# A hybrid attention encoder: order of weight roundings, a later place for weight loads, and small edits at both ends

## The chip, the cores and the metric

The kernel runs on one core of one Trainium2 chip. The metric is the device time of one execution in microseconds. Before the change, three runs took 1371.48, 1372.12 and 1373.95 us; their median, 1372.12 us, is the time before.

The engines are called as in the profile: PE multiplies matrices, ACT, DVE and POOL work on vectors, and SP only issues transfers (DMAs). Each works through its own queue in order.

## The reference, cut to what matters

Two layers work on 512 tokens of width 1024, and a final norm follows. Each layer adds three things to x:

```
for l in range(DEPTH):                                   # DEPTH = 2
    x = x + hybrid_mixer(rms_norm(x, norm_mix[l]), ...)  # 8 neighbourhood heads || 8 grouped-query heads
    x = x + memory_cross_attention(rms_norm(x, norm_mem_q[l]), rms_norm(mem, norm_mem_kv[l]), ...)
    x = x + conv_ffn(rms_norm(x, norm_ffn[l]), ...)      # SwiGLU, width-3 convolution, 2816 channels
return rms_norm(x, norm_final)
```

The neighbourhood attention (NA) has windows of 8 x 16 on an 8 x 64 grid of tokens, with a learned bias. The grouped-query attention (GQA) has 8 query heads on 2 key heads, with normed and rotated queries and keys. The memory attention has 4 heads over 256 memory tokens. All inputs are float32.

## The kernel before, in words

**Splitting.** A matmul takes operands in a rounded 32-bit format (`fp32r`). To keep float32's accuracy each operand is split into a rounded part `hi` and a rest `lo`, and each product is three matmuls (`mm3`): hi·hi, hi·lo, lo·hi. So each weight tile goes through three steps: a DMA of the raw tile on SP's queue (`emit_raw`), a rounding copy on ACT (`act.copy`, L290), and a subtraction, on POOL for nearly all tiles and on DVE for a few (`tensor_sub`, L291). There are two raw buffers and four pairs of `hi` and `lo`. A raw buffer comes free when the subtraction has read it, and the DMA for the next tile, which waits for that, holds up SP's queue.

**Plan and prefetch.** `plan` lists the weight tiles of the whole run in order of use. `get_w(key)` hands out the next one; before that it splits tiles until two (`AHEAD`) lie ready beyond it, and issues raw loads until two more (`N_RAW`) are on their way.

**Order.** PE's and SP's instructions stay in program order (`InOrder`, `Counted`). ACT's, DVE's and POOL's are ordered by a planner, which simulates a timeline and takes what is ready there, by priority: `behind(n)` gives a later rank (negative: an earlier one), and `tc.issue_after(ins)` forces an instruction behind another on its engine. The roundings have rank `behind(45)`, and `follow()` forces them behind the first of the reads of PSUM by ACT (`read(...)`) that were traced since the `get_w` before. The roundings of some tiles are forced behind the last closing row of x instead (`closed`), and those of `w_up` and `w_down` are not forced.

**Stages of a layer.** First some steps of projections (`attn_fill.step(N_FIRST[l])`: 7 in layer 0, 16 in layer 1; a step of a query or key projection is 6 matmuls of 512 columns, one of a value projection 12 of 256 columns). Then a weave of the NA units (8) and one of the GQA units (16), whose scores, softmax, transposes and value products are interleaved on PE with the remaining projections as filler. Then the rest of the filler, the memory attention with its own weave, and the feed-forward part in three groups of channels. `late(n, fn)` puts off a piece of program text until PE has been given n times 3.6 us of estimated work (`LATE = 3600`): so come the copies of each key half to the other half of the partitions (`double`, `r<-r`, two DMAs), the value blocks that straddle two tiles (`straddle`, `r<-r`, five DMAs), the swap for the rotation (`t<-t`, four DMAs) and others.

**Banks.** PSUM has four `mm` banks (projections, value products), two `sc` (scores) and two `tr` (transposes, statistics). `mem_stat`, in layer 0's NA weave, computes the memory's norm with two `tr` banks.

**The start.** `FIRST` gives the order in which chunks of x and pieces of the first three weights are loaded. ACT's queue issues the first norm's gains (`par`), then the first pieces of weights 0 and 1; SP's queue issues the rest. Six products of `ident` warm PE up.

**The end.** `down_last` works in two halves of 256 tokens. After the last row of a half its norm's `stat` sums the squares of the first seven chunks with PE, then those of the last one; then come a power on POOL, `spread` (products with `ident` that spread the result over the partitions), the scaling and the stores.

Of the kernel before, what the change touches and what calls it, by code (L numbers as in the profile page):

```python
# [13 lines left out]
ALU = mybir.AluOpType  # L14
# [4 lines left out]
P = 128  # L19
S = 512  # L20
D = 1024
# [7 lines left out]
MB = MEMN // P  # L29
# [3 lines left out]
EPS = 1e-6  # L33
# [16 lines left out]
MEM_FILL = [1, 1, 2, 2, 1, 3, 1, 3, 1, 3, 1]  # L50
N_ROWS = 3
LATE = 3600
W_BEHIND, N_RAW, N_W, AHEAD, AHEAD_HELD, N_WARM, N_LATE, N_FIRST = 45, 2, 4, 2, 5, 6, 4, (7, 16)


class InOrder:
# [113 lines left out]
def weave(n, steps, filler, quanta):  # L170


    last = max(st[0] for st in steps if st)
    for s in range(n + last):
        pieces = iter(quanta(s))
        for st in steps:
            if st is None:
                filler(next(pieces))
            elif 0 <= s - st[0] < n:
                st[1](s - st[0])  # L180
# [3 lines left out]
def encoder_kernel(ctx: ExitStack, tc: tile.TileContext, t: dict, out: bass.AP):  # L184
    nc = tc.nc
    PE, SP = Counted(tc, nc.tensor), InOrder(tc, nc.sync)
    late = Late(PE)
    ACT_IN_ORDER = InOrder(tc, nc.scalar)
    ACT, DVE, POOL = Free(nc.scalar), Free(nc.vector), Free(nc.gpsimd)
# [9 lines left out]
    @contextmanager  # L199
    def behind(n):  # L200


        at = tc.cur_priority
        tc.cur_priority = at + n
        yield
        tc.cur_priority = at
# [30 lines left out]
    ps_mm = lambda: ps("mm", 4)  # L237
    ps_s = lambda: ps("sc", 2)
    ps_t = lambda: ps("tr", 2)
# [6 lines left out]
    closed = []  # L246


    reads, marks = [], [0, 0]

    def read(e):
        reads.append(e.ins)
# [1 line left out]

    def follow():
        at = marks[-2]
        return tc.issue_after(reads[at]) if at < len(reads) else nullcontext()

    def raw_tile():
        key, loads, nk, ncol, eng = plan[len(raws)]  # L260
# [7 lines left out]
    def emit_raw():  # L268
        raw, loads = raw_tile()
        for dst, src in loads:  # L270
            SP.dma_start(dst(raw), src)
# [22 lines left out]
    def get_w(key, ahead=AHEAD):  # L294
        n = done[0]
        assert plan[n][0] == key, (plan[n][0], key)
        marks.append(len(reads))
        ahead = n + 1 + ahead
        while ahead < min(len(plan), n + 1 + AHEAD_HELD) and plan[ahead][4][1:] == "r":
            ahead += 1  # L300
        while len(ready) < min(len(plan), ahead):
            while len(raws) < min(len(plan), len(ready) + N_RAW):
                emit_raw()
            emit_split()
        while len(raws) < min(len(plan), len(ready) + N_RAW):
            emit_raw()
        done[0] += 1
        w = ready[n]
        ready[n] = None
        return w  # L310
# [73 lines left out]


    FIRST = [0, (0, 0, 2), 1, (1, 0, 2), 2, (0, 2, 4), 3, (1, 2, 4), (2, 0, 4), 4, (0, 4, 8), 5, (1, 4, 8), (2, 4, 8), 6, 7]
    nc.scalar.dma_start(par[:, 0, 0:8], t["par"][:, 0, 0:8])
    first_loads = []
    for n in FIRST:
        if isinstance(n, int):  # L390
            SP.dma_start(xT[n], t["xT"][n * P : (n + 1) * P, :])
            continue
        u, k0, k1 = n
        if u == len(first_loads):
            first_loads.append(raw_tile())
        raw, loads = first_loads[u]
        (nc.scalar if u < 2 and k0 == 0 else SP).dma_start(raw[:, k0:k1], loads[0][1][:, k0:k1])
    ACT_IN_ORDER.copy(small(1), ones)
    qkg = cpool.tile([P, DEPTH, 2], F32, name="qkg")
    gfin = cpool.tile([P, KC], F32, name="gfin")  # L400
# [37 lines left out]
    class Norm:  # L438
# [41 lines left out]
                eng.tensor_add(self.acc, self.acc, sq)  # L480
            return e

        def stat(self, factor=1.0):
            nb = self.n // P

            def sums(sq):
                pv = ps_t()
                for b in range(nb):
                    PE.matmul(pv[:, b : b + 1], sq[:, b * P : b * P + P], ones, start=True, stop=True)
                return pv[:, 0:nb]  # L490

            if self.last is None:
                self.rstd, self.var = rsqrt(sums(self.acc), nb, 1.0 / D, factor)
                return

            part, v, self.rstd = small(nb), small(nb), small(nb)
            DVE.tensor_scalar(part, sums(self.acc), 1.0 / D, EPS, op0=ALU.mult, op1=ALU.add)
            DVE.scalar_tensor_tensor(v, sums(self.last), 1.0 / D, part, op0=ALU.mult, op1=ALU.add)
            POOL.tensor_tensor(self.rstd, v, mhalf[:, :nb], op=ALU.pow)

        def spread(self, copy=ACT.copy):
# [65 lines left out]
    def mem_stat():  # L567

        acc = None
        for i in range(KC // 2):  # L570
            sq = tmp((2, MEMN))
            SP.dma_start(sq, t["memT"][i * 256 : (i + 1) * 256, :].rearrange("(k p) n -> p k n", p=P))
            yield
            ACT.activation(sq, sq, AF.Square)
            if acc is None:
                acc = sq
            else:
                POOL.tensor_add(acc, acc, sq)
        POOL.tensor_add(acc[:, 0], acc[:, 0], acc[:, 1])
        yield  # L580
        pv = ps_t()
        for b in range(MB):
            PE.matmul(pv[:, b : b + 1], acc[:, 0, b * P : (b + 1) * P], ones, start=True, stop=True)
        v = small(MB)
        DVE.tensor_scalar(v, pv[:, 0:MB], 1.0 / D, EPS, op0=ALU.mult, op1=ALU.add)
        POOL.tensor_tensor(mem_rstd, v, mhalf[:, :MB], op=ALU.pow)
        yield
        pr = ps_t()
        for b in range(MB):
            PE.matmul(pr[:, b * P : (b + 1) * P], mem_rstd[:, b : b + 1].to_broadcast([P, P]), ident,  # L590
                      start=True, stop=True)
        with behind(-30):
            ACT.copy(mem_rep, pr[:, :MEMN])
        yield

    warm = ps_t()
    for _ in range(N_WARM):
        PE.matmul(warm[:, 0:P], ident, ident, start=True, stop=True)  # L600
    nn = Norm(G_MIX, 0)
    DVE_IN_ORDER = InOrder(tc, nc.vector)
    for n in FIRST:
# [3 lines left out]
        u, k0, k1 = n  # L607
# [22 lines left out]
    for l in range(DEPTH):  # L630
# [465 lines left out]
        def na_quanta(s):  # L1096
# [4 lines left out]
            if s == 3:  # L1101
# [2 lines left out]
                gqa_eps()  # L1104
            return [NA_FILL] * 3

        weave(8, [(2, na_transpose), None, (1, na_normalise), (0, na_scores), None, (2, na_values), None], attn_fill.run, na_quanta)
        weave(4 * NB, [(2, gqa_transpose_p), (1, gqa_normalise), (0, gqa_scores), (3, lambda u: gqa_values(u, 0)),
                       (4, lambda u: gqa_values(u, 1)), None], attn_fill.pace, lambda s: [GQA_SLOT[s]])
        attn_fill.finish()  # L1110
        nn = nns[0]

# [184 lines left out]
        def down_last(g):  # L1297

            j0, nj = GROUPS[g]
            ops = [acts.pop(j) for j in range(j0, j0 + nj)]  # L1300
            ws = []

            def scale(half, m):
                xc = xT[m][:, 256 * half : 256 * half + 256]
                DVE.tensor_scalar(xc, xc, gfin[:, m : m + 1], 1.0, op0=ALU.mult, op1=ALU.mult)

            def finish(norm, last=False):
                norm.spread()
                y = [rtile((4, 256), F32) for _ in range(2)]
                for k in range(KC):  # L1310
                    yk, xk = y[k // 4][:, k % 4], xT[k][:, norm.cols]
                    if k in (2, 5):
                        POOL.tensor_mul(yk, xk, norm.rep)
                    else:
                        DVE.tensor_mul(yk, xk, norm.psum)
                for i, (k, n) in enumerate(((0, 2), (2, 2), (4, 2), (6, 1), (7, 1))):
                    (ACT_IN_ORDER if last and i % 2 else SP).dma_start(
                        out[k * P : (k + n) * P, norm.cols].rearrange("(k p) n -> p k n", p=P), y[k // 4][:, k % 4 : k % 4 + n])

            norms = []  # L1320
            for half in range(2):
                cs = slice(256 * half, 256 * half + 256)
                hops = [(hi[:, cs], lo[:, cs]) for hi, lo in ops]
                norms.append(Norm(cols=cs))
                rows = []
                for m in range(KC):
                    if half == 0:
                        ws.append(get_w(("down", g, m)))
                    rows.append(ps_mm()[:, :256])
                    late = half == 0 and m < N_LATE  # L1330
                    gemm_T(rows[m], ws[m], hops, range(nj - 1 if late else nj), 0, nj - 1)
                    for i in [m] if not late else range(N_LATE) if m == N_LATE - 1 else []:
                        if late:
                            gemm_T(rows[i], ws[i], hops, [nj - 1], 0, nj - 1)
                        DVE.tensor_add(xT[i][:, cs], xT[i][:, cs], rows[i])
                        norms[half].square(i)
                        scale(half, i)
                    if half == 1 and m == 1:
                        norms[0].stat()
                    elif half == 1 and m == 3:  # L1340
                        finish(norms[0])
            norms[1].stat()
            finish(norms[1], True)

        for g, (j0, nj) in enumerate(GROUPS):
# [96 lines left out]
```

## Time and profile before

| | us |
|---|---|
| median of three runs | 1372.12 |
| the profiled execution | 1373.07 |
| its span, first to last instruction | 1371.3 |
| PE busy | 1347.8 |
| DVE, POOL, ACT busy | 881.6, 688.4, 675.3 |

In this profile a row of the timeline has the start, the length, the engine and line of the program, the operation, what it writes and reads, its shape and count; brackets show how long the engine was idle before it and what ended that. A wait is listed as the one who waits, the one that released it, the total in us, the number of times and the longest. A busy time by stretch has the stretch, its length, then the busy time of PE, PEld (weight load), DVE, ACT and POOL with counts, the granted share of the PE clock, the share of the DMA engines and GB/s. A DMA issue has the size and the median time until it landed. Most float32 products have two records for each instruction.

### The profile page before, as it was taken

The numbers are of one execution on the slowest core, as the hardware profiler recorded it, in microseconds if no ns is written. First come the engines' busy times: TensorE is split into PE (matmuls) and PEld (weight loads), VectorE is DVE, ScalarE is ACT, GpSimd is POOL, SyncE is SP. The second block draws the span as 40 slices with busy tenths as digits, with TensorE's granted clock in tenths as the row PEclk, the third lists the DMA queues.
The fourth block names the chain that finished last, engine by engine and source line by source line (L and its number), as shares of the span: only waits on it lengthen the run. The fifth ranks groups of instructions, "written<-read, shape, count | busy, mean of one in ns | idle before, by whom it ended". The sixth has DMA issues, their size and how long they took to land.

```text
span 1371.3 us, 19217 instructions
## 1 busy us (share of the span) xinstructions
PE 1347.8 (98%) x7068; PEld 1154.7 (84%) x7068; DVE 881.6 (64%) x1542; ACT 675.3 (49%) x1258; POOL 688.4 (50%) x491
## 2 busy tenths in 40 slices
PE   9999999999999999999989999999999999999997
PEld 7888899878888888888878888998788888888897
DVE  6677775665885288177436677746758834862874
ACT  6776676555542244243447667756554422432441
POOL 2467756627444444443734576657264444444451
PEclk9999999999999999999999999999999999999998
DMA  6763213313333332432355441132143333323321
GB/s 214 208 187 102 59 47 93 108 46 104 97 92 98 102 93 81 118 93 81 100 148 174 137 116 54 59 97 93 32 123 92 99 101 93 100 85 108 96 89 62
DMA packets 219358, 139.88 MB, mean 102 GB/s; under 512 B 6144, under 2 KB 212224, under 8 KB 219264
## 3 DMA queue, kind: packets, MB, share of 16 engines
q1 hardware_dynamic: 218160, 137.99, 34.1%
q8 instruction: 56, 0.92, 0.3%
q10 hardware_dynamic: 1104, 0.66, 0.2%
q14 instruction: 38, 0.31, 0.1%
HBM read 126.05 MB, written 2.10 MB: 93 GB/s over the span
## 4 chain that ended last, share of the span: by engine, by line
PE 89%; ACT 4%; DVE 3%; DMA 2%; issue 1%; SPq 0%; ACTq 0%; POOL 0%; DVEq 0%
PE mm L77 79%; PE sc L77 6%; PE tr L64 3%; PE tr L77 1%; ACT t L790 1%; DMA r<-r 1%; ACT hi L290 1%; DMA t<-in_memT 1%; DMA xT<-in_xT 0%; DVE sc L784 0%; DVE t L480 0%; DMA raw<-in_w_in 0%; ACT t L1145 0%; DVE r L727 0%; ACT r L725 0%
## 5 line engine op out<-in xcount | busy, mean ns | idle before, releaser
L291 POOL TENSOR_TENSOR lo<-raw,hi 128x1024 fp32r<-128x1024 f32 (+2 forms) x268 | 500.3, 1877 | 486.5 <-ACT hi L290 471.9
L77 PE MATMUL mm<-xg,hi 128*128 128x512 f32 x1920 | 595.2, 391 | 0.0
L77 PEld LDWEIGHTS mm<-xg,hi 128*128 128x128 f32 x1920 | 355.7, 188 | 70.1
L77 PE MATMUL mm<-xg,lo 128*128 128x512 f32 x960 | 373.8, 389 | 0.0
L290 ACT CAST hi<-raw 128x512 fp32r<-128x512 f32 (+2 forms) x276 | 224.2, 836 | 297.8 <-PE mm L77 251.7
L77 PE MATMUL mm<-r,hi 128*128 128x512 f32 (+1 forms) x1096 | 316.3, 373 | 0.0
L77 PEld LDWEIGHTS mm<-r,hi 128*128 128x128 f32 x1096 | 198.3, 189 | 34.5 <-DVE r L507 0.4
L1266 DVE SCALAR_TENSOR_TENSOR t<-t,par,t 128x7 f32<-128x7 f32 (+1 forms) x352 | 202.0, 641 | 34.0 <-ACT t L1259 34.0
L77 PEld LDWEIGHTS mm<-xg,lo 128*128 128x128 f32 x960 | 180.2, 188 | 38.2
L77 PE MATMUL mm<-r,lo 128*128 128x512 f32 (+1 forms) x548 | 203.6, 372 | 0.0
L77 PEld LDWEIGHTS mm<-r,lo 128*128 128x128 f32 x548 | 103.3, 188 | 18.0
L1251 DVE TENSOR_TENSOR t<-mm,rep 128x512 f32<-128x512 f32 x88 | 60.1, 687 | 78.7 <-PE mm L77 62.4
L513 POOL TENSOR_SCALAR t<-t,s 128x512 f32<-128x512 f32 (+1 forms) x112 | 66.7, 611 | 81.6 <-DVE s L796 41.7
L1272 DVE TENSOR_TENSOR r<-t,r 128x512 fp32r<-128x512 f32 x44 | 90.4, 2054 | 7.3 <-ACT r L1271 4.1
L1268 ACT ACTIVATE t<-t 128x512 f32<-128x512 f32 x44 | 27.8, 633 | 134.5 <-DVE t L1266 134.4
L1295 DVE TENSOR_TENSOR xT<-xT,mm 128x512 f32<-128x512 f32 x32 | 21.9, 686 | 106.8 <-PE mm L77 106.8
L77 PE MATMUL sc<-r,r 128*128 128x256 f32 (+1 forms) x352 | 71.6, 336 | 4.9 <-DMA r<-r 4.4
L1259 ACT ACTIVATE t<-t,par 128x512 f32<-128x512 f32 x88 | 66.8, 806 | 3.3 <-DVE t L1251 3.3
L64 PE MATMUL tr<-ident,t 128*128 128x128 f32 x456 | 61.5, 273 | 5.7 <-DVE t L513 3.9
L64 PEld LDWEIGHTS tr<-ident,t 128*128 128x128 f32 x456 | 52.5, 140 | 14.5 <-issue 6.0
L77 PE MATMUL mm<-r,r 128*128 128x256 f32 (+1 forms) x428 | 62.2, 297 | 1.3 <-DMA r<-r 1.3
L77 PEld LDWEIGHTS sc<-r,r 128*128 128x128 f32 x352 | 52.6, 193 | 9.8 <-DMA r<-r 4.4
(154 smaller groups left out, 1624.2 us busy)
## 6 DMA issues: line engine op xcount, KB each, us to landing
raw<-in_w_up SPq DMA_DIRECT2D x88, 512.0 KB, 3.7
raw<-in_w_in SPq DMA_DIRECT2D x33, 512.0 KB, 4.1
raw<-in_w_down SPq DMA_DIRECT2D x32, 448.0 KB, 3.7
raw<-in_w_mem_kv SPq DMA_DIRECT2D x16, 512.0 KB, 3.9
raw<-in_w_down SPq DMA_DIRECT2D x16, 512.0 KB, 3.9
r<-in_bias SPq DMA_DIRECT2D x16, 384.0 KB, 5.5
r<-r SPq DMA_DIRECT2D x22, 256.0 KB, 5.6
raw<-in_w_out SPq DMA_DIRECT2D x8, 512.0 KB, 4.2
```

The lines of the kernel that those rows point to most:

```text
L64: return lambda *a, **k: self.tc.keep_in_program_order(op(*a, **k))
L77: return self.tc.keep_in_program_order(self.engine.matmul(out, lhsT, rhs, **k))
L290: act.copy(hi[:, k], raw[:, k])
L291: (POOL if eng[0] == "P" else DVE).tensor_sub(lo[:, k], raw[:, k], f(hi)[:, k])
L513: eng.tensor_scalar(e, e, sums[:, col : col + 1], 1.0, op0=ALU.mult, op1=ALU.mult)
L790: ACT.activation(es[j][:, i, :], sc[j][:, i, :], AF.Exp, bias=nmx[:, col], scale=-1.0, accum_out=sums[:, col])
L1251: DVE.tensor_mul(u, us[side], ffn.rep)
L1259: ACT.activation(cc, u, AF.Identity, bias=par[:, l, CB + ch : CB + ch + 1], scale=w[1])
L1266: DVE.scalar_tensor_tensor(cc[:, dst], u[:, src], wi, cc[:, dst], op0=ALU.mult, op1=ALU.add)
L1268: ACT.activation(cs[0], cs[0], AF.Silu)
L1272: DVE.tensor_sub(acts[j][1], cs[0], f(acts[j][0]))
L1295: DVE.tensor_add(xT[m], xT[m], pm)
```

## The change

- `follow()` forces the roundings only while `woven[0]` is true, that is during the two weaves of the attentions; before, it did so everywhere outside the feed-forward part.
- During the weaves `get_w` no longer issues its last raw loads at once, but with `late(1, load)`; what a split needs is still loaded before it.
- `mem_stat` takes `mm` banks instead of `tr` banks, and its first DVE operation gets an earlier rank.
- The first piece of weight 0 is issued on ACT's queue before `par`; the first piece of weight 1 moves to SP's queue, behind the second chunk of x.
- 7 warm-up products instead of 6; in layer 0, 8 steps of projection before the NA weave instead of 7.
- In the last norm three products of `ident` follow the sums of the first seven chunks and three more the sums of the last.

```
-W_BEHIND, N_RAW, N_W, AHEAD, AHEAD_HELD, N_WARM, N_LATE, N_FIRST = 45, 2, 4, 2, 5, 6, 4, (7, 16)
+W_BEHIND, N_RAW, N_W, AHEAD, AHEAD_HELD, N_WARM, N_LATE, N_FIRST = 45, 2, 4, 2, 5, 7, 4, (8, 16)
...
-    reads, marks = [], [0, 0]
+    reads, marks, woven = [], [0, 0], [False]
...
     def follow():
         at = marks[-2]
-        return tc.issue_after(reads[at]) if at < len(reads) else nullcontext()
+        return tc.issue_after(reads[at]) if woven[0] and at < len(reads) else nullcontext()
...
-        while len(ready) < min(len(plan), ahead):
+        def load():
             while len(raws) < min(len(plan), len(ready) + N_RAW):
                 emit_raw()
+
+        while len(ready) < min(len(plan), ahead):
+            load()
             emit_split()
-        while len(raws) < min(len(plan), len(ready) + N_RAW):
-            emit_raw()
+
+        if woven[0]:
+            late(1, load)
+        else:
+            load()
...
-    nc.scalar.dma_start(par[:, 0, 0:8], t["par"][:, 0, 0:8])
...
-        (nc.scalar if u < 2 and k0 == 0 else SP).dma_start(raw[:, k0:k1], loads[0][1][:, k0:k1])
+        (nc.scalar if n == FIRST[1] else SP).dma_start(raw[:, k0:k1], loads[0][1][:, k0:k1])
+        if n == FIRST[1]:
+            nc.scalar.dma_start(par[:, 0, 0:8], t["par"][:, 0, 0:8])
...
-        def stat(self, factor=1.0):
+        def stat(self, factor=1.0, warm=lambda: None):
...
             DVE.tensor_scalar(part, sums(self.acc), 1.0 / D, EPS, op0=ALU.mult, op1=ALU.add)
+            warm()
             DVE.scalar_tensor_tensor(v, sums(self.last), 1.0 / D, part, op0=ALU.mult, op1=ALU.add)
+            warm()
...
-        pv = ps_t()
+        pv = ps_mm()
...
-        DVE.tensor_scalar(v, pv[:, 0:MB], 1.0 / D, EPS, op0=ALU.mult, op1=ALU.add)
+        with behind(-30):
+            DVE.tensor_scalar(v, pv[:, 0:MB], 1.0 / D, EPS, op0=ALU.mult, op1=ALU.add)
...
-        pr = ps_t()
+        pr = ps_mm()
...
+    def warm_up(n):
+
+        warm = ps_t()
+        for _ in range(n):
+            PE.matmul(warm[:, 0:P], ident, ident, start=True, stop=True)
+
+    warm_up(N_WARM)
...
+        woven[0] = True
         weave(8, ...)
         weave(4 * NB, ...)
+        woven[0] = False
...
-            norms[1].stat()
+            norms[1].stat(warm=lambda: warm_up(3))
```

More of the change, by code (lines that the diff above doesn't have):

```diff
@@ L594, in mem_stat @@
         yield
-    warm = ps_t()
-    for _ in range(N_WARM):
-        PE.matmul(warm[:, 0:P], ident, ident, start=True, stop=True)
+    def warm_up(n):
[3 more added lines that the diff above has]
+    warm_up(N_WARM)
     nn = Norm(G_MIX, 0)
```

## The prediction

> **What bounds the kernel now.** I read the page first, then PE's waits, then each longer wait in the timeline, then the granted clock beside it.
>
> ```profile
> PE 1347.8 (98%) x7068; PEld 1154.7 (84%) x7068; DVE 881.6 (64%) x1542; ACT 675.3 (49%) x1258; POOL 688.4 (50%) x491
> PE sc L77 <- DMA r<-r: 4.4, 2, 4.2
> PE tr L64 <- DVE t L513: 3.9, 4, 1.6
> PE mm L77 <- DMA r<-r: 1.3, 1, 1.3
> ```
>
> TensorE is busy for 98% of the span, so no other engine's load matters as such, and the change adds nothing to PE's work but seven small warm-up products. What it can win or lose lies in the other 2%: the list of PE's waits (microseconds in total, times, longest) names the pieces of it, and the work of the others counts only where it ends one of them. The largest is one wait of 4.2 us for an `r<-r` transfer, at the start of layer 1's attentions:
>
> ```profile
> 710.33 0.80 PE L77 MATMUL sc<-r,r 128*128 128x256 f32 x2 [4.24 <-DMA r<-r]
> 711.35 1.62 PE L77 MATMUL sc<-r,r 128*128 128x256 f32 x6 [0.21 <-DMA r<-r]
> 710.33:715.40 5.07, 4.85 (x21) 4.59 (x22) 1.68 (x8) 3.12 (x9) 2.47 (x2) 0.52 0.51 150
> 715.40:720.00 4.60, 4.60 (x41) 4.60 (x40) 0.66 (x2) 1.64 (x5) 1.39 (x3) 1.00 0.97 255
> ```
>
> The first two rows are of the timeline (start, length, engine and line; in brackets PE's idle time before and what ended it), the others are busy times by stretch, where the third number from the end is the granted clock. The wait costs more than itself: afterwards the clock is 0.52 for 5.07 us. In that stretch 21 matmuls ran; at the 4.60/41 = 0.112 us of the next stretch they would take 2.36, so 5.07 - 0.21 - 2.36 = 2.5 us go to the slow clock. The whole event is worth 4.24 + 0.21 + 2.5 = 6.95 us, 0.5% of the run.
>
> **Term A, the roundings before layer 1's attentions: -6.4 us.** Why was that transfer late?
>
> ```profile
> 696.07 1.18 ACT L707 CAST r<-sc 64x512 fp32r<-64x512 f32 x2
> 699.83 1.18 ACT L725 CAST r<-mm 64x512 fp32r<-64x512 f32 x2 [2.59 <-DVE mm L693]
> 701.03 1.14 ACT L290 CAST hi<-raw 128x512 fp32r<-128x512 f32 x2
> 701.73 2.55 POOL L291 TENSOR_TENSOR lo<-raw,hi 128x512 fp32r<-128x512 f32 x2 [11.86 <-ACT hi L290]
> 697.66 1.41 DVE L711 TENSOR_TENSOR r<-sc,r 64x512 fp32r<-64x512 f32 x2
> 688.92 9.10 SPq L64 DMA_DIRECT2D raw<-in_w_in  x2
> 697.65 7.02 SPq L64 DMA_DIRECT2D raw<-in_w_in  x2
> 705.07 1.17 SPq L64 DMA_DIRECT2D r<-r  x2
> raw<-in_w_in SPq DMA_DIRECT2D x33, 512.0 KB, 4.1
> ```
>
> The key halves to be doubled were written by DVE at 699.07 (697.66 + 1.41). Their transfers stand on SP's queue behind a raw weight load that waits for its buffer, that is for POOL's subtraction, which ends at 704.28; the subtraction waits for the rounding at 701.03, and POOL had idled 11.86 us. The rounding was tied behind the read at 699.83. These are steps 1 to 16 of layer 1, before the two weaves, where the tie now goes. The weight's load was issued at 688.92 and a load of this kind lands after 4.1 us (the last row, from the list of DMA issues), so at 693.0. Free of the tie, the rounding either starts then (POOL done at 693.0 + about 0.6 for the first half + 2.55 = 696.2, the doubling issued when its source is ready, 699.1) or after the reads of 696.07, at 697.3 (POOL done at 700.5, doubling at 701.3, as 705.07 follows 704.28 by 0.8). The doubling lands about 5.2 us after issue (705.07 to 710.33, less a little): 704.3 or 706.5. PE asks at 706.1 (710.33 - 4.24). So nothing remains, or some 0.4 us, and about as much again for the second half (the two doublings share the 1.17 us of issue), without a slow clock: gain 6.95 or 6.0, taken 6.4; bounds 0 (the order stays) and 6.95. Next late would be the second key's doubling, which is needed only by the next head pair, after PE has gone through another stretch of fill. One untied rounding in layer 0's first steps comes back in term G. Outside the weaves the tie also goes in the memory attention, term D. In the up and down projections it was never used.
>
> **Term B, raw loads a step later in the weaves: -1.3 us.** Per weight one load of 0.37 us issue moves by 3.6 us of PE work, behind the key doublings, value straddles, query swaps, bias and memory loads that are queued in that time. One wait shows the price of the old order:
>
> ```profile
> 768.30 2.54 POOL L291 TENSOR_TENSOR lo<-raw,hi 128x512 fp32r<-128x512 f32 x2
> 770.86 0.37 SPq L64 DMA_DIRECT2D raw<-in_w_in  x1
> 771.33 3.26 SPq L64 DMA_DIRECT2D r<-r  x5
> 777.05 1.22 PE L77 MATMUL mm<-r,r 128*128 128x256 f32 x6 [1.29 <-DMA r<-r]
> ```
>
> Five straddles stand behind a load that waited for POOL until 770.84. Two of the five read the first half of the values, ready long before, so they can leave early and the other three follow some 1.3 us sooner, with no 512 KB load ahead of them. Bounds 0 and -1.3, the whole wait; taken -1.3, since SP had nothing else to do between. The cover of the later loads is the slack of the weights, weighed below as a rival.
>
> **Term C, the memory statistic in `mm` banks: -0.9 us.**
>
> ```profile
> 85.44 0.63 PE L64 MATMUL tr<-ident,t 128*128 128x128 f32 x4 [1.09 <-DVE s L585]
> 96.90 0.33 PE L64 MATMUL tr<-ident,t 128*128 128x128 f32 x1 [0.28 <-ACT mem_rep L593]
> 83.43 0.48 DVE L510 SCALAR_TENSOR_TENSOR r<-mm,s,r 128x256 fp32r<-128x256 f32 x1 [1.07 <-ACT r L509]
> 85.77 0.87 DVE L838 TENSOR_TENSOR t<-mm,t 64x256 f32<-64x256 f32 x2
> ```
>
> The two waits, 1.37 us, are for `tr` banks held by the statistic; they go. But when the statistic's products come, just ahead of the transposes and so near 83.4, the four `mm` banks are all held: two by the value products (read by DVE until 86.6), one by a projection in progress, one until 83.91. So the statistic would wait 0.5 us itself, with transposes and projection queued behind it on PE. Bounds -1.4 and +0.5.
>
> **Term D, roundings in the memory attention: -1.2 us.**
>
> ```profile
> 288.75 0.33 DVE L513 TENSOR_SCALAR s<-s,s 128x1 f32<-128x1 f32 x2
> 288.83 0.59 ACT L506 CAST r<-tr 128x512 fp32r<-128x512 f32 x1 [1.68 <-PE tr L64]
> 289.31 1.05 ACT L290 CAST hi<-raw 128x1024 fp32r<-128x1024 f32 x1
> 290.27 0.56 ACT L1145 ACTIVATE t<-sc,s,s 128x256 f32<-128x256 f32 x1
> 293.16 0.63 PE L64 MATMUL tr<-ident,t 128*128 128x128 f32 x4 [1.60 <-DVE t L513]
> ```
>
> The exponent was ready at 289.08 and ran at 290.27, after a tied rounding of 1.05 us; the transposes then waited 1.60, and as much again once more (the four waits for L513 sum to 3.9, the longest 1.6), which I read as the same place in layer 1. ACT had 1.68 us idle before 288.83, room for that rounding. If it moves there, 1.2 us return in each layer; if it lands before another exponent, up to 1.05 is lost. Half of 2.4 is taken; bounds -3.2 and +1.1.
>
> **Term E, the warm end: -0.5 us.**
>
> ```profile
> 1350.42 0.60 PE L77 MATMUL tr<-ident,s 128*128 128x128 f32 x4
> 1362.12 0.61 PE L77 MATMUL tr<-ones,t 128*128 128x1 f32 x4 [0.68 <-ACT t L469]
> 1363.76 1.22 PE L77 MATMUL tr<-ident,s 128*128 128x128 f32 x4 [1.03 <-POOL s L499]
> 1363.70:1365.00 1.30, 1.22 (x4) 0.93 (x4) 0.00 (x0) 0.00 (x0) 0.00 (x1) 0.52 0.00 0
> ```
>
> The same four records took 0.60 at 1350.42 and 1.22 at the end, at clock 0.52. Three products of two records are some 0.7 to 0.9 us (0.60/4 x 6), put into gaps of 0.68 and 1.03. The first set may overrun by 0.2, and DVE, POOL, ACT and the stores all follow it. Bounds -0.6 and +0.2. The Trainium skill ("TensorE: Matmul & The Clock Gate", section "HAM oscillation — how this bites in real kernels") says that the clock survives idle gaps under about 3.4 us; by that rule these gaps need no warming and the term would be 0, the time 1362.7. The row disagrees: the clock was halved after gaps of 0.68 and 1.03. After the 4.24 us gap of term A rule and row agree.
>
> **Terms F and G, the beginning: -0.1 and +0.5 us.**
>
> ```profile
> 17.16 6.48 DVE L480 TENSOR_TENSOR t<-t,t 128x512 f32<-128x512 f32 x6
> 37.70 0.95 PE L77 MATMUL sc<-r,r 128*128 128x256 f32 x6 [0.48 <-DVE r L713]
> 39.03 0.38 PE L77 MATMUL mm<-hi,xg 128*128 128x256 f32 x1 [0.39 <-DVE r L727]
> ```
>
> F: the first weight piece leaves ACT's queue one issue sooner, the norm's gains behind it one later, and the second weight piece moves to SP's queue, behind two chunks of x. Whatever PE saves is taken back by the sum of squares, which DVE ends at 23.64 and PE already awaits: -0.1, bounds -0.3 and +0.3. The seventh warm-up product lies in PE's idle time. G: one more half block of values (twelve products of some 0.12 us, 1.4 us) before the weave covers the 0.48 wait, but the block that now waits 0.39 us for a bank, freed just before 39.03, then comes before the scores, which begin some 0.4 us ahead of that 0.48 wait, near 36.8; it waits up to 2.2 us, 1.3 more than the two waits now. A rounding of 1.14 us, untied, may leave ACT's reads of the same stretch and shorten that. Bounds -0.9 and +1.5; taken +0.5.
>
> Sum: -6.4 - 1.3 - 0.9 - 1.2 - 0.5 - 0.1 + 0.5 = -9.9 us. The profiled execution took 1373.07 us, 0.95 above the median 1372.12 of the runs shown, so the median is forecast at 1362.2.
>
> **Rivals.** First, the order stays: the untied rounding is still put behind the read of the second query (699.83), because ACT's order is a planner's. Then A is 0 and the time 1368.6. For it: the planner gives these roundings a late rank. Against: ACT idles 2.59 us before 699.83.
>
> Second, on the other side, weights come too late. SP's loads slip by 3.6 us and by what is now ahead of them:
>
> ```profile
> 57.56 0.37 SPq L64 DMA_DIRECT2D raw<-in_w_in  x1
> 66.92 2.55 POOL L291 TENSOR_TENSOR lo<-raw,hi 128x512 fp32r<-128x512 f32 x2
> 75.55 0.40 PE L77 MATMUL mm<-hi,xg 128*128 128x256 f32 x2
> ```
>
> This load is of the second half of a value weight, first used near 75.6; its low part is done at 69.47, a slack of 6.1 us. With ten projections in each layer, a slip of 7.5 us would cost 1.4 us at each of 20: +28, time 1390. It decides from a slip of 6.1 + (9.9 + 2.7)/20 = 6.7 us. Against: landed by 61.7 (57.56 + 4.1), this weight lies there for 5 us before its subtraction, so most of a slip is absorbed ahead of the slack; and no wait of PE for POOL's low parts stands in the list of before.
>
> **Numbers.** Forecast 0.69 (1357.5 to 1366); order stays 0.13 (faster, 1368.6); small losses of C, D and G eat most, without A, 0.06 (within 0.2%, 2.7 us, about what a measurement can tell); late weights 0.12 (slower). Faster 0.82. All good ends together are -14.7, 1357.4; the range 1357.5 to 1369.5 holds the first two cases and leaves out the last two.
>
> **What would show it.** A: no `sc` wait for `r<-r` near 705 and clock 1.00 there; B: none at 775; C: no wait for L585, perhaps one for a `mm` bank; D: shorter waits for L513; E: last `tr<-ident` near 0.6; G: a wait for L727 before the first scores. New PE waits for `lo` would prove me wrong.

## The result, and the profile after

The changed kernel took 1367.49 us (median of 6 runs, 1365.69 to 1370.78), the kernel before beside it 1372.7 us: a ratio of 0.9962, 95% interval 0.9949 to 0.9976. It is faster, by 5.2 us where 9.9 were forecast. The profiled execution took 1367.86 us, with a span of 1366.1 (before 1373.07 and 1371.3).

The page's busy times and the list of PE's waits (total, times, longest, in us) of the changed kernel:

```profile
PE 1349.0 (99%) x7082; PEld 1157.5 (85%) x7082; DVE 877.3 (64%) x1542; ACT 675.0 (49%) x1258; POOL 688.1 (50%) x491
PE mm L77 <- ACT t L903: 2.4, 1, 2.4
PE mm L77 <- DVE r L740: 1.4, 1, 1.4
PE tr L77 <- POOL ident masks.py:199: 1.3, 1, 1.3
PE mm L77 <- ACT r L518: 1.3, 1, 1.3
PE sc L77 <- ACT xg L64: 1.0, 1, 1.0
PE tr L64 <- DVE t L522: 0.9, 3, 0.3
...
PE tr L64 <- DVE xg L516: 0.7, 1, 0.7
PE tr L64 <- DVE s L967: 0.6, 1, 0.6
PE tr L77 <- POOL s L508: 0.2, 1, 0.2
```

Both waits for `r<-r`, 4.4 and 1.3 us, have left the list. The waits for the softmax scaling in the memory attention (L513 before, L522 now) shrank from 3.9 to 0.9, and the one for the end's statistic from 1.0 to 0.2. But the list also has three new waits of `mm` products, 2.4, 1.4 and 1.3 us, for banks that ACT or DVE must first empty.

Rows of the timeline of the changed kernel at the places of terms A, B and E (start, length, engine; SPq is SP's queue), and the busy times by stretch at the places of A and E (granted clock third from the end):

```profile
704.01 1.25 SPq L64 DMA_DIRECT2D r<-r  x2
711.53 0.64 PE L77 MATMUL sc<-r,r 128*128 128x256 f32 x4
710.00:715.00 5.00, 5.00 (x44) 5.00 (x43) 3.40 (x11) 4.91 (x9) 3.51 (x3) 1.00 0.01 3
763.07 6.97 SPq L64 DMA_DIRECT2D r<-r  x5
1356.61 0.91 PE L77 MATMUL tr<-ident 128*128 128x128 f32 x6
1359.06 0.71 PE L77 MATMUL tr<-ident,s 128*128 128x128 f32 x4 [0.25 <-POOL s L508]
1359.00:1359.90 0.90, 0.71 (x4) 0.52 (x4) 0.00 (x0) 0.01 (x1) 0.01 (x1) 1.00 0.00 0
```

The key doubling is issued at 704.01 and the scores that need it start at 711.53 without a wait, at clock 1.00. The five straddles are issued before the next raw load. At the end the warm products stand in the gaps, and the last spread takes 0.71 at clock 1.00 instead of 1.22 at 0.52; whether they are the reason is taken up at e5.

What took back half of the gain lies in layer 0's GQA weave. The timeline there, on PE and ACT, and then the busy times by stretch around it:

```profile
117.88 0.71 PE L77 MATMUL mm<-r,r 128*128 128x256 f32 x4
120.32 0.60 ACT L903 ACTIVATE t<-mm 128x512 f32<-128x512 f32 x1 [1.65 <-DVE t L902]
120.97 0.74 PE L77 MATMUL mm<-r,r 128*128 128x256 f32 x4 [2.38 <-ACT t L903]
```

```profile
36.00:44.00 8.00, 6.59 (x55) 6.39 (x55) 6.48 (x16) 3.90 (x11) 2.51 (x2) 1.00 0.52 152
86.00:92.00 6.00, 4.71 (x40) 4.50 (x39) 3.90 (x10) 4.54 (x11) 3.56 (x6) 1.00 1.04 297
122.60:129.20 6.60, 6.60 (x26) 5.82 (x25) 2.12 (x5) 1.78 (x4) 5.32 (x5) 0.50 0.54 169
```

A value product at 118.6 finds its bank still holding a finished projection of the GQA, which ACT reads last, at 120.32, behind DVE's scaling. The wait is 2.38 us, and then the clock is 0.50 for 6.6 us, which costs another 6.6 x (1 - 0.50) = 3.3. So this one place costs 5.7 us in this execution. The waits of 1.41 near 38 and 1.29 near 87 leave the clock at 1.00.

### The profile page after: what moved, and what is told of

It reads as the page before. It is cut to its first block, busy times and chain, and to the rows that moved or that the text cites. A ratio compares the mean times of both kernels' runs of the same rounds, so it can differ in the third digit from the quotient of the medians.

```text
span 1366.1 us, 19239 instructions
## 1 busy us (share of the span) xinstructions
PE 1349.0 (99%) x7082; PEld 1157.5 (85%) x7082; DVE 877.3 (64%) x1542; ACT 675.0 (49%) x1258; POOL 688.1 (50%) x491
## 4 chain that ended last, share of the span: by engine, by line
PE 91%; DVE 3%; ACT 3%; DMA 2%; issue 1%; SPq 0%; POOL 0%; DVEq 0%; ACTq 0%
PE mm L77 80%; PE sc L77 6%; PE tr L64 3%; PE tr L77 1%; DMA raw<-in_w_in 1%; DMA t<-in_memT 1%; ACT t L803 1%; ACT hi L290 0%; SPq L64 0%; DMA xT<-in_xT 0%; DVE t L487 0%; ACT r L515 0%; DVE sc L797 0%; DVE r L740 0%; ACT r L738 0%
## 5 line engine op out<-in xcount | busy, mean ns | idle before, releaser
L522 POOL TENSOR_SCALAR t<-t,s 128x512 f32<-128x512 f32 (+1 forms) x112 | 66.8, 610 | 78.0 <-DVE s L809 36.8
L77 PEld LDWEIGHTS mm<-r,r 128*128 128x128 f32 x428 | 56.3, 191 | 5.1 <-ACT t L903 2.6
```

Source lines behind the costliest of these rows:

```text
L77: return self.tc.keep_in_program_order(self.engine.matmul(out, lhsT, rhs, **k))
L522: eng.tensor_scalar(e, e, sums[:, col : col + 1], 1.0, op0=ALU.mult, op1=ALU.mult)
```

## The experiments

Three theories were set up for the missing gain. Theory 1: the eighth first step shifts the projections against the value products by half a block, so that more `mm` banks are wanted than the four there are. Theory 2: the memory's statistic in `mm` banks crowds them. Theory 3: the later raw loads change the order in layer 0. Every kernel was timed beside the kernel before, and ratios are to that.

**e1: seven first steps.** The changed kernel with

```
-... N_FIRST = 45, 2, 4, 2, 5, 7, 4, (8, 16)
+... N_FIRST = 45, 2, 4, 2, 5, 7, 4, (7, 16)
```

> The changed kernel with 7 first steps in layer 0 instead of 8, nothing else. Theory 1 (the eighth step): it moves every projection of layer 0's first weave by half a block against the value products, so that a fifth mm bank is wanted; the new waits of PE at 37 us (1.41), 86 us (1.29) and 118 us (2.38) go, about 4.5 us, 1363 us. Theory 2 (the statistic's mm banks): the wait at 86 us stays or moves, the one at 118 us stays; 1366 to 1367. Theory 3 (later loads make ACT and DVE late): both stay, 1367.

Measured: 1363.23 us, ratio 0.992 (0.9908 to 0.9932); span 1362.0, 4.1 below the changed kernel's. The waits at 118 and 87 are gone, the one at 38 is back to two small ones. In their place stand one of 0.77 at 129 and a longer one, in the timeline of e1 at 60 us (with busy times by stretch as the last row):

```profile
56.86 0.63 ACT L583 ACTIVATE t<-t 128x512 f32<-128x512 f32 x1
58.74 2.56 DVE L291 TENSOR_TENSOR lo<-raw,hi 128x512 fp32r<-128x512 f32 x2
61.94 0.68 DVE L516 TENSOR_TENSOR r<-tr,r 128x512 fp32r<-128x512 f32 x1
62.68 0.74 PE L77 MATMUL mm<-r,r 128*128 128x256 f32 x4 [2.36 <-DVE r L516]
63.80:66.80 3.00, 3.00 (x9) 2.33 (x8) 1.77 (x5) 2.89 (x10) 0.00 (x0) 0.50 1.07 359
```

Theory 1 holds for the waits. That the time also meets the 1363 expected is luck, for the sum held neither the new wait nor any slow clock: DVE's low part of a weight and two score operations stand ahead of what PE awaits, and the clock falls again, to 0.50 for some 3 us.

**e2: the memory's statistic back in `tr` banks.** The changed kernel with

```
-        pv = ps_mm()
+        pv = ps_t()
...
-        pr = ps_mm()
+        pr = ps_t()
```

> The changed kernel with the memory statistic back in tr banks (early DVE rank kept). Theory 1: the wait at 118 us stays, the one at 86 us goes or shrinks and the tr waits of before (1.09 and 0.28) come back in part: 1367, within 1 us of the changed kernel. Theory 2: the waits at 86 and 118 us both go, 3.7 us less, 1364.

Measured: 1367.88 us, ratio 0.9954 (0.994 to 0.9967). The list of PE's waits of e2:

```profile
PE tr L64 <- DVE s L595: 2.6, 1, 2.6
PE mm L77 <- ACT t L903: 2.4, 1, 2.4
```

The wait at 118 stays, and the one for an `mm` bank near 87 only becomes one for a `tr` bank. Theory 2 falls. In this execution the clock stays 1.00 after both waits, so its span, 1364.3, is below the changed kernel's.

**e3: raw loads at once again.** The changed kernel with

```
-        if woven[0]:
-            late(1, load)
-        else:
-            load()
+        load()
```

> The changed kernel with the raw loads at once in the weaves too. Theories 1 and 2: the waits at 86 and 118 us stay, and the wait for the straddles near 771 us (1.29) comes back: 1368.5 to 1369. Theory 3: the waits at 86, 118 and 163 us go (5 us) and 1.3 come back: 1364.

Measured: 1366.98 us, ratio 0.9952 (0.9937 to 0.9967). The waits for banks stay (2.73 and 1.31) and the wait for straddles is back, 0.86. The timeline of e3 at the longest wait, with the stretch around it:

```profile
120.81 0.74 PE L77 MATMUL mm<-r,r 128*128 128x256 f32 x4 [2.73 <-ACT t L900]
118.00:130.00 12.00, 9.28 (x52) 7.92 (x52) 7.94 (x14) 6.44 (x13) 10.46 (x11) 1.00 0.32 86
```

The wait is longer than the changed kernel's, and yet the clock does not fall. So the wait comes from the eighth step, but the slow clock behind it does not always follow. With eight steps, the place of the loads hardly matters; theory 3 is not what explains the wait at 118.

**e4: untied roundings alone.** The kernel before with only the `woven[0]` condition in `follow()`, and `woven[0]` true during the weaves: terms A and D.

> The kernel before with the roundings tied in the weaves only, nothing else. If terms A and D are as the traces of before and after show them (the doubling's wait with its slow clock 6.95, the memory attentions' waits 2.6 to 3), it is 9 to 10 us faster: 1363, and the losses of the changed kernel come from its other parts. If untying itself moves work in layer 0 so that it waits there, it gains no more than the changed kernel, 5 us: 1367.

Measured: 1362.98 us, ratio 0.9917 (0.9904 to 0.993), span 1361.2, 10.1 us below that of before. This one edit is worth more than the whole change. In its list of PE's waits the one of the scores for `r<-r` is gone, the straddles' has 1.2 and the scaling in the memory attention 0.9.

**e5: e4 and the warm end.** e4 with `warm_up` and

```
-            norms[1].stat()
+            norms[1].stat(warm=lambda: warm_up(3))
```

> The kernel with the roundings tied in the weaves only (run e4), with the three and three warm-up products in the last norm added. If the end's slow clock is gone and the first set costs nothing, 1.2 to 1.7 us less than e4, by 0.1% or a little over, 1361.5 beside 1363; the waits before the last sums and the last spread (0.68 and 1.02) shrink. Rival: the products only fill the waits, and the last spread still takes 1.2 us: the same as e4.

Measured: 1362.31 us, ratio 0.9913 (0.9899 to 0.9926), span 1.1 below e4's. The medians differ by 0.7 us, less than the 1.2 to 1.7 expected, and the intervals overlap. The end of e4, without the warm products, and that of e5 (timeline and busy times by stretch):

```profile
1354.18 0.71 PE L77 MATMUL tr<-ident,s 128*128 128x128 f32 x4 [1.02 <-POOL s L499]
1354.10:1355.00 0.90, 0.71 (x4) 0.52 (x4) 0.00 (x0) 0.00 (x0) 0.02 (x1) 1.00 0.00 0
1353.12 0.71 PE L77 MATMUL tr<-ident,s 128*128 128x128 f32 x4 [0.25 <-POOL s L501]
```

The last spread of e4 also takes 0.71, at clock 1.00, after the same gaps as in the kernel before. From the first sums of the squares to this spread both kernels take 2.8 us, so the 1.1 us between the spans arise before the end. Term E's gain is therefore not shown: the products fill the waits and nothing gets shorter, much as the rival said, though both expectations had taken 1.2 us for e4's spread. Of the kernels without them, before and e12 have 1.22 there and e4, e8, e9 and e11 0.71; all eight kernels with them have 0.71, which leaves open whether they prevent a slow clock that comes only at times.

**e6: seven steps, raw loads at once.** The edits of e1 and e3 together.

> The changed kernel with 7 first steps and the raw loads at once. In run e1 (7 first steps, later loads) PE waited 2.36 us at 60 us for DVE, where a weight's subtraction stood ahead of a transpose's. If the later loads put it there, this wait goes here and the straddles' wait (1.0 to 1.3) comes back: about 1 us faster than e1, 1362. If the planner puts it there for another reason, the wait stays and the time is 1364.

Measured: 1362.49 us, ratio 0.9911 (0.9898 to 0.9925). Against e1 the wait at 60 shrinks from 2.36 to 0.12, and waits for straddles of 0.94 and 0.21 return. Why e1's was so long is seen on SP's queue and ACT. In e6's timeline:

```profile
58.94 0.37 SPq L64 DMA_DIRECT2D raw<-in_w_in  x1
59.37 0.50 SPq L64 DMA_DIRECT2D t<-in_memT  x1
56.84 0.59 ACT L512 CAST r<-tr 128x512 fp32r<-128x512 f32 x1
```

and in e1's:

```profile
50.49 0.37 SPq L64 DMA_DIRECT2D t<-in_memT  x1
59.09 0.37 SPq L64 DMA_DIRECT2D raw<-in_w_in  x1
57.51 0.59 ACT L515 CAST r<-tr 128x512 fp32r<-128x512 f32 x1
```

With the raw load put off, a chunk of the memory no longer stands behind it and leaves 8.9 us sooner. Its squares on ACT (L583, 56.86 in e1) then come ahead of the rounding of the transposed probabilities (L515), and DVE's part of that slides behind two score operations. A queue that gets free sooner had brought other work forward, into a crowded place. Why the planner then puts the score operations first, the traces do not show.

**e7: tied again in layer 1's first steps.** The changed kernel, where `follow()` also forces while

```
+        tied[0] = l == 1
         attn_fill.step(N_FIRST[l])
+        tied[0] = False
```

> The changed kernel with the roundings tied again in layer 1's 16 first steps alone. If term A is right, the wait of 4.2 us for the key doubling near 703 us and the clock of 0.52 behind it come back: 7 us more than the changed kernel, 1374, slower than before by 0.1%. If something else removed that wait (the loads queued later), it stays away: 1367.5.

Measured: 1373.01 us, ratio 0.9992 (0.9983 to 1.0001). The wait is back in the timeline of e7, with a slow clock in the busy times by stretch:

```profile
713.76 0.80 PE L77 MATMUL sc<-r,r 128*128 128x256 f32 x2 [3.52 <-DMA r<-r]
714.97 1.62 PE L77 MATMUL sc<-r,r 128*128 128x256 f32 x6 [0.41 <-DMA r<-r]
712.50:717.00 4.50, 2.83 (x11) 2.57 (x12) 0.81 (x5) 2.42 (x3) 2.53 (x3) 0.53 0.91 275
```

Term A is confirmed: without it the changed kernel is no faster than the one before. Its span is 5.2 above the changed kernel's, and not 7, at least in part because the slow clock behind the wait at 118 lasts only some 3.4 us here, against 6.6 there.

**e8: later raw loads alone.** The kernel before with `late(1, load)` during the weaves, roundings tied as before.

> The kernel before with the raw loads queued a step later in the weaves, nothing else. Term B: the wait for the straddles near 775 us (1.29) goes, 1.3 us less, ratio 0.999. Rival: it reorders ACT and DVE in layer 0's first weave, and PE waits there for mm banks or operands; then 1 to 3 us are lost and it is no faster than before. The wait at 706 us stays in both.

Measured: 1375.34 us, ratio 1.0007 (0.9999 to 1.0016). From the list of PE's waits of e8:

```profile
PE mm L77 <- DVE r L512: 2.5, 1, 2.5
```

The straddles' wait of 1.29 is gone in layer 1, but layer 0 pays the same wait as e1, 2.54 at 60 us, and one more of 1.0 (L876). Term B over both layers is no gain.

**e9: the eighth step alone.** The kernel before with `N_FIRST` of (8, 16).

> The kernel before with one edit, eight first steps in layer 0 instead of seven. My theory (the eighth step shifts the projections against the value products by half a block, so that five banks are wanted where there are four) expects it slower by about 4 us, 1377 to 1379, with waits of PE for a bank held by a finished projection near 118 us (about 2.4) and 86 us (about 1.3). The rival, that the step only does harm together with the later loads or the untied roundings, expects no change (within 0.1%) and neither wait.

Measured: 1381.68 us, ratio 1.0056 (1.0042 to 1.007): 8.0 us slower, twice what theory 1 had expected. The timeline of e9 at the three places, each with a stretch of slow clock that comes with it:

```profile
38.97 0.39 PE L77 MATMUL mm<-hi,xg 128*128 128x256 f32 x1 [2.04 <-DVE r L727]
40.00:43.20 3.20, 3.20 (x17) 3.20 (x16) 2.02 (x8) 0.00 (x0) 0.00 (x0) 0.50 0.94 293
90.57 0.63 PE L64 MATMUL tr<-ident,t 128*128 128x128 f32 x4 [2.40 <-DVE s L585]
91.20:94.40 3.20, 3.20 (x17) 3.20 (x17) 1.03 (x2) 1.30 (x3) 0.04 (x2) 0.50 1.06 244
125.80 1.23 PE L77 MATMUL mm<-r,r 128*128 128x256 f32 x4 [2.49 <-ACT t L890]
125.40:128.60 3.20, 2.80 (x9) 2.42 (x10) 1.67 (x4) 2.12 (x5) 2.69 (x3) 0.50 0.33 82
```

All three waits came with the step alone, so it needs no help from the loads or the roundings; and in this execution the clock was 0.50 for some 3 us at each, which the expectation had left out.

**e10: seven steps, raw loads later in layer 1 only.** The changed kernel with `N_FIRST` of (7, 16) and

```
-        if woven[0]:
+        if woven[0] == 2:
             late(1, load)
...
-        woven[0] = True
+        woven[0] = l + 1
```

> The kernel after with seven first steps, and with the raw loads a step later in layer 1's weaves only. If the later loads cost only by the order that they give layer 0's first weave, the wait near 60 us (2.36 with seven steps and later loads everywhere) is at most 0.2, and the waits for straddles near 770 (0.94 and 0.21 with seven steps and loads at once) are gone: about 1361.4, some 1 us below the 1362.49 of loads at once. The rival, that the later loads only exchange one wait for another wherever they are, expects 1362.5 or more, with a new wait of 0.5 to 2.5 us in layer 1's weaves.

Measured: 1359.61 us (1358.92 to 1359.95), ratio 0.9895 (0.9882 to 0.9909), span 1357.5: the fastest kernel of this study, ahead of both the kernel before and the changed one. The two longest entries in its list of PE's waits:

```profile
PE tr L77 <- POOL ident masks.py:199: 1.3, 1, 1.3
PE mm L77 <- DVE r L519: 1.1, 2, 0.7
```

Neither the wait at 60 nor those for straddles are there. So term B's mechanism holds in layer 1, and its cost lies in layer 0. The gain over e6 is larger than the 1.15 us of the straddles' waits for another reason: the spans differ by 3.3, of which 2.1 are there by the first value projection (32.22 in e6, 30.14 here), where e6 waits 0.88 for the sum of squares (0.3 here) and its clock is then 0.50 from 25 to 28 us. The edits of the two kernels leave that place alone.

**e11: the statistic in `mm` banks alone.** The kernel before with both `ps_t()` of the statistic turned into `ps_mm()` and its first DVE operation under `behind(-30)`.

> The kernel before with one edit, the memory's statistic in the banks of the projections and its first operation on DVE earlier. My forecast of the step expects a gain of 0.9 us (the waits of 1.09 near 85 us and of 0.28 near 97 us gone, 0.5 for a bank at 83). The rival, that the statistic crowds out the value products, expects no gain or a loss of up to 1 us, with a wait for a bank of 1 us or more between 83 and 90 us.

Measured: 1373.23 us, ratio 0.9994 (0.9985 to 1.0003), which shows neither gain nor loss. The timeline of e11 at the place:

```profile
83.47 0.35 PE L77 MATMUL mm<-hi,xg 128*128 128x256 f32 x1 [0.47 <-DVE r L510]
85.81 0.58 PE L77 MATMUL mm<-ones,t 128*128 128x1 f32 x4 [0.68 <-DVE r L510]
```

The waits of 1.09 and 0.28 for `tr` banks went, and 0.47 and 0.68 for `mm` banks came: 0.2 us remain of the 0.9 forecast.

**e12: nine first steps.** The kernel before with `N_FIRST` of (9, 16).

> The kernel before with nine first steps in layer 0 instead of seven. If what costs is the half block by which the projections are shifted, nine steps (a shift by a whole block) cost less than eight: within 1.5 us of the kernel before, without a wait over 1 us near 118 us. If any earlier step costs, because the weaves then lack filler or their order gets worse, nine cost as much as eight or more, 4 us or over.

Measured: 1379.37 us, ratio 1.0041 (1.0029 to 1.0054): 5.7 us slower. The timeline of e12, with one stretch:

```profile
39.87 0.39 PE L77 MATMUL mm<-hi,xg 128*128 128x256 f32 x1 [2.04 <-DVE r L727]
42.00:47.00 5.00, 5.00 (x43) 4.96 (x42) 2.20 (x10) 2.48 (x8) 0.00 (x0) 1.00 1.06 291
80.43 0.35 PE L77 MATMUL mm<-hi,xg 128*128 128x256 f32 x1 [1.38 <-DVE t L838]
148.20 1.41 PE L77 MATMUL sc<-r,r 128*128 128x512 f32 x4 [2.14 <-ACT t L948]
```

Near 120 no long wait is left, as expected of a shift by a whole block; but others come instead, and the loss is within the rival's 4 us or over. After none of these waits does the clock fall, not even after 2.14; 0.9 of the 5.7 us are lost ahead of the first value projection (31.93, before 31.07). So the half block explains the wait at 118 and not the price as a whole: seven steps fit the weaves' order, eight and nine do not, each for its own reasons.

## Why the prediction was right and wrong

The direction was right, the size was not: 5.2 us against 9.9. Step by step, in us of span or of waits:

| term | forecast | measured |
|---|---|---|
| A, roundings before layer 1's attentions | -6.4 | -6.9: the wait and the slow clock are gone; put back in e7, +5.2 of span |
| B, later raw loads | -1.3 | -1.3 at 775; over both layers alone no gain (e8) |
| C, statistic's banks | -0.9 | -0.2 (e11's waits) |
| D, memory attention | -1.2 | -3.0 (waits 3.9 to 0.9) |
| E, warm end | -0.5 | -0.5 (last spread 1.22 to 0.71), but e4 has 0.71 without it: not shown |
| F, start | -0.1 | +0.3 (first wait 0.7 to 1.0); not resolved, the same start reaches the first value projection at 30.14 (e10) to 32.22 (e6) |
| G, eighth step | +0.5 | alone +8.0 (e9); taken out of the changed kernel, 4.1 of span (e1) |

For the changed kernel as a whole, the waits add up so: -6.9 - 1.3 - 3.0 - 0.5 + 0.3, then +5.7 at 118, +0.5 at 38 (1.41 for 0.48 and 0.39), -0.1 at 87 (1.29 for 1.09 and 0.28), +1.0 near 164 (0.67 and 0.57 for 0.28): -4.3 of the 5.2 by which the spans differ; 0.9 is spread too thinly to name.

The step that failed is term G, whose bounds of -0.9 and +1.5 did not hold its price. Its mechanism at 38 us was right: a wait for the bank freed by L727 comes before the first scores (1.41, where up to 2.2 was reckoned). But the prediction followed the step only to the first scores. A step more at the front moves every later projection in two weaves against the units' products, and the dearest collision came 80 us further on. And it priced a wait at its length, though the fence that term A rests on already showed that a long wait can cost half as much again in clock. Of the 5.7 us at 118, 2.4 are the wait that the step was not reckoned to cause and 3.3 the clock, which e2 and e3 did not lose in their traces. The Trainium skill ("TensorE: Matmul & The Clock Gate", section "HAM oscillation — how this bites in real kernels") gives as its rule "no PE-idle gaps >~3.4µs"; the trace of the changed kernel disagrees with it as a limit below which the clock is safe, with 0.50 after 2.38, while e3's, with 1.00 after 2.73, does not.

Term D was the right mechanism, mis-sized: I took half of the 2.4 that a rounding moved into ACT's idle time would bring, for fear that it would land ahead of another exponent; no wait over 0.3 for the scaling is left in either layer. Term B was right where it was read, in layer 1, and I looked for its cost only in late weights. No wait of PE for low parts of weights appeared, so that rival fell; the cost lies in layer 0 (e10), and by the rows of e1 and e6 it came from a memory chunk that was let through sooner. Term E rested on one execution: the slow clock at the end of the kernel before came again in e12, but not in e4, e8, e9 or e11, which have the same gaps, so there may have been nothing to gain. Term C named the wait that would replace the old ones, 0.5 for a bank; e11 has 0.47 and a second one of 0.68 behind it. The rival that the order stays fell: the doubling moved as reckoned, and e7 shows what it is worth. The rival of small losses had the right direction for C and G, but not for D, and A's gain, which it left out, came.

What is not settled: which of the collisions with eight or nine steps could be mended by another order of the readers (for instance ACT's L903 sooner). That was not tried. Nor is it known why the clock fell after the wait at 118 in the changed kernel and not in e2 and e3.

## What to carry to other kernels

An edit that moves the start of a stream of filler moves all of it against the work it is woven with: follow it to the end of the weave and count the banks wanted at each crossing, instead of costing the first place alone. Putting off a transfer does not only make it later, it lets what stood behind it go sooner, and that work has to fit where it lands. Price a wait of some 2.4 us with the clock that it may cost, and look at the same place in other traces before a gain or a loss is put down to the clock. Test the parts of a bundle alone: here one part was worth twice the whole.

## What the runs showed of the hardware

Where a slow stretch is read closely, the granted clock is 0.50. It was lost after much shorter waits than I had reckoned with: 0.50 for 6.6 us after 2.38 us idle, and for some 3 us after 2.36 (e1) and with the waits of 2.04, 2.40 and 2.49 (e9). But it stayed 1.00 after 2.04 and 2.14 in e12, after 2.37 and 2.59 in e2, and after 2.73 in e3. In e6 it was 0.50 from 25 to 28 us after a wait of only 0.88, followed by eight records of one-column products. After the longest waits for the key doubling, from 3.52 (e7) to 4.24 us (before), it was lost in all six kernels that have one. So at 2 to 2.7 us of idle time the length of the wait does not decide; what does, no run here shows.

One program can fare either way. Of e2's six executions three have a mean granted clock of 0.999 and take 1365.94 to 1367.15 us, and three have 0.995 or 0.996 and take 1368.60 to 1370.81. The end shows the same from kernel to kernel: after equal gaps of 0.68 and about 1.03 the last spread took 1.22 us in two traces and 0.71 in four.
